# Rank-160 gate products with the activations stationary, split gate weights, and a re-drawn instruction order in a four-layer hybrid trunk

## The chip, the cores and the metric

The kernel runs on one core of one Trainium2 chip. The metric is the device time of one execution in microseconds (us); the time of a kernel is the median of its runs. TensorE's granted clock is 1.00 of full speed (2.4 GHz) in every stretch of the profile.

## The reference

The input x is 256 tokens by 1024 features in float32. Four layers follow each other; each is a token mixer and a SwiGLU feed-forward block, both with RMSNorm ahead and a residual add behind. The mixers are, in order, RWKV-7 (layer 0), stick-breaking attention (layer 1), top-64 sparse attention (layer 2) and RWKV-7 again (layer 3). What matters here, cut from the reference:

```
g = sigmoid(xg @ g1) @ g2                       # g1: 1024 x 160, g2: 160 x 1024, both RWKV layers
v = v + (v_first - v) * sigmoid(v0 + (xv @ v1) @ v2)    # v1: 1024 x 32, v2: 32 x 1024, layer 3 only
y = (groupnorm(y) + bonus) * g ; out = y @ w_out

# stick breaking: z = q k^T; att = exp(log_sigmoid(z) + sum of log_sigmoid(-z) over the later keys)
```

`xg` and `xv` are mixes of each token with the one before it. The RWKV recurrence is computed in chunks of 64 tokens, with a triangular inverse of each chunk.

## The kernel before, in words

Features lie on the 128 partitions, tokens (256) along the free axis. A float32 product that must be exact is done in one of two ways. Either both operands stay float32, and TensorE spends two MATMUL records on each product. Or the weight piece (128x1024, 512 KB) is split into a rounded float32r part `wh` and a rest `wl` (`piece`, line 825: one DMA into `raw`, one cast, one VectorE subtraction), the activation likewise, and three float32r products are summed (`mm3`). `raw`, `wh` and `wl` have three buffers each.

**The order** of all instructions on all engines is worked out in Python before the program is built. Every instruction is recorded as an operation with a cost; `Plan.schedule` (line 685) places them by list scheduling on a cost model, with the longest remaining path as priority, in 16 rounds (`ROUNDS`, line 221), and keeps the best. One more round then adds random shifts to the priorities of ranges of operations (`_nudge`, line 673), from a table of seeds, ranges and widths (`NUDGES`, line 223, 84 entries). An operation marked "any" goes to ScalarE or VectorE as the planner finds room. Where TensorE would be idle, the planner puts in small dummy products (tile `warm_o`).

**The gate in `rwkv`.** Its first weights lie in the tile `lora` (line 1034), which shares its memory with the later key tile `QC` (line 1181): `QC` can be written only when the gate's first products have read `lora`. For each of the 8 feature chunks, `g1a` (128 columns of g1) and `g1b` (the other 32, doubled to fill 64) are stationary and `xg` moves, 256 columns, in float32 (line 1142 on); in layer 3 the 64 columns of v1 (doubled) are a third product, on the other half of the array. The results are copied out to `sg` and go through a sigmoid. The second half (tile `pg`, line 1331 on) multiplies by g2: four DMAs of 128 KB and one of 256 KB fetch it (`lg`, `lg1`, lines 1259 and 1263), and for each of 4 pairs of chunks there are two full float32 products and two of 32 rows, four copies in all of 256 columns going to `gT`. `gT` is first used when the recurrence's output is scaled.

**What surrounds it.** In order of dependence: mixes; the products k (`kp`) and r (`rp`); the small products that make decay and rate; the keys `QC` (written twice by one VectorE instruction, line 1198: slots 0 and 2 hold the same values) and `PR`; scores `sc`, masked into `SB`; then a trip through DRAM (`scr`), 31 steps of a triangular inverse on VectorE (`inv`), back through DRAM (`scx`) into `XT`, whose two tiles take one `wh` and one `wl` buffer; `cmb` completes the inverse; then the chain of small products over the chunks (`xu`, `qu`, `Y`, `pS`), the norm, and the output product `po`. The value products `vp` and the gate's second half lie beside the inverse.

**In `stick`**, per head, two float32r products with the triangle `ntri` and one float32 product with `nones` (line 1543) make the sums over later keys.

Of the kernel before, what the change touches and what calls it, by code (L numbers as in the profile page):

```python
# [22 lines left out]
P = 128  # L23
# [4 lines left out]
C = 64  # L28
# [21 lines left out]
CONSTS = [("ident", 128), ("bones", 128), ("center", 128), ("mstrict", 64), ("mincl", 64),  # L50
# [138 lines left out]
class Queue:  # L189
# [33 lines left out]
NUDGES = [  # L223
# [21 lines left out]
]  # L245
# [64 lines left out]
class Plan:  # L310
# [362 lines left out]
    def _nudge(self):  # L673

        shift = collections.Counter()
        for seed, lo, hi, width in NUDGES:
            draw = random.Random(seed)
            for o in self.ops[max(lo, 0):hi]:
                d = draw.gauss(0.0, width)
                if draw.random() < 0.5:  # L680
                    shift[o] += d
        for o, d in shift.items():
            o.rank += d

    def schedule(self, counts):
# [6 lines left out]
        for k in range(ROUNDS + 1):  # L692
            if k == ROUNDS:
                order = [o for o, _, _ in basis]
                for o, start, end in basis:
                    o.start, o.end = start, end
            base = [(o, o.start, o.end) for o in order]
            self._place(counts, order)
            if k == ROUNDS:
                self._nudge()  # L700
# [4 lines left out]
            if r is None:  # L705
                break
# [46 lines left out]
def trunk(ctx: ExitStack, tc: tile.TileContext, xT_in, vecs_in, wts, lora_in, consts_in, id32_in, nqk_in, outT, order, layers=None):  # L753
# [96 lines left out]
    def split(h, l, src):  # L850
        anye.copy(h, src)
        dve.tensor_tensor(l, src, f(h), op=ALU.subtract)

# [179 lines left out]
    def rwkv(j, layer, after):  # L1033
        lw = T([4096], "QC", "lora")
        sp.dma_start(lw[:, :1024], lora_in[j][:, :1024])
        sp.dma_start(lw[:, 1024:], lora_in[j][:, 1024:4096])
        w1a1, l2 = v3(lw[:, :1024], 8), lw[:, 1024:2048]
        g1a, g1b = v3(lw[:, 2048:3072], 8), v3(lw[:, 3072:], 8)
# [103 lines left out]
        pga, pgb = bank("g1a"), bank("g1b")  # L1142
        for c in range(NC):
            xg = xm("mg", c)
            mixed = plan.ops[-1]
            if sv_:
                x = xm("mv", c)
                split(xv[0][:, c], xv[1][:, c], x)
            else:
                x = xv[:, c]  # L1150
                mix(x, "mv", c)
            with unit(1, 1010.0):
                pe.matmul(pga[:, :S], g1a[:, c, :], xg, start=(c == 0), stop=(c == NC - 1))
                pe.matmul(pgb[:64, :S], g1b[:, c, :64], xg, start=(c == 0), stop=(c == NC - 1))
                if j == 1:
                    pe.matmul(pgb[64:, :S], g1b[:, c, 64:], x, start=(c == 0), stop=(c == NC - 1))
        anye.copy(sga, pga[:, :S])
        anye.copy(sgb if j == 1 else sgb[:64], pgb[:, :S] if j == 1 else pgb[:64, :S])
# [25 lines left out]
        for p in range(0, NC, 2):  # L1184
# [13 lines left out]
            dve.tensor_tensor(pairs(QC, p)[:, :, ::2], c8(kk)[:, :, None].to_broadcast([P, 2 * NCH, 2, C]),  # L1198
                              c8(Ft[:, p:p + 2])[:, :, None].to_broadcast([P, 2 * NCH, 2, C]), op=ALU.mult)
# [58 lines left out]
        act.activation(sgb[:64], sgb[:64], AF.Sigmoid)  # L1258
        lg = [T([S], "xm", "lg") for i in range(4)]
        for i in range(4):  # L1260
            sp.dma_start(lg[i], lora_in[j][:, 4096 + i * S:4096 + (i + 1) * S])
            plan.after(plan.ops[-1], [mixed])
        lg1 = T([2 * S], "sqa", "lg1")
        sp.dma_start(lg1, lora_in[j][:, 5120:5120 + 2 * S])

        def second(out, p, r0, stop):

            r = slice(r0 + (p % 2) * 32, r0 + (p % 2) * 32 + 32)
            pe.matmul(out, lg1[r, (p // 2) * P:(p // 2 + 1) * P], sgb[r], start=(r0 > 0), stop=stop)

        for n in range(4):
# [7 lines left out]
            with unit(2):  # L1279
                for i in range(2):  # L1280
                    second(pv_[i][:, :S], 2 * n + i, 64, True)
# [49 lines left out]
        gT = T([NC, S], "s7", "gT")  # L1331
        for p in range(0, NC, 2):
            pg = bank("pg"), bank("pg")
            with unit():
                for i in range(2):
                    pe.matmul(pg[i][:, :S], lg[p // 2][:, i * P:(i + 1) * P], sga, start=True, stop=False)
                for i in range(2):
# [159 lines left out]
    def stick(layer, after):  # L1497
# [3 lines left out]
        msb, ntri = T([P], "kc0", "msb", BF16), T([P], "kc1", "ntri", F32R)  # L1501
        pool.tensor_copy(msb, cst("msb"))
        anye.copy(ntri, cst("ntri"))
        ohl = [T([2, 4, S], f"s{h}", "ohl", F32R) for h in range(2)]
# [5 lines left out]
        for p in range(8):  # L1510
# [22 lines left out]
            for hh in range(2):  # L1533
# [6 lines left out]
                with unit():  # L1540
                    pe.matmul(z[:, :W3], ntri, eh, start=False, stop=False, skip_group_check=True)
                    pe.matmul(z[:, :W3], ntri, el, start=False, stop=False, skip_group_check=True)
                    pe.matmul(z[:, P:S], cst("nones"), e[:, S:], start=False, stop=True, skip_group_check=True)
# [241 lines left out]
def _piece(d, key):  # L1785

    k = key[0]
    if k in "gu":
# [34 lines left out]
def _npieces(layers=None):  # L1823
    return sum({"rwkv": 32, "stick": 32, "dsa": 37, "ffn": 66}[k] for k, _ in _subs(layers))


def _lora(d, j):
# [4 lines left out]
    last = np.zeros((4, 32, PIECE), np.float32)  # L1832
    for k, w in enumerate((g2[128:], v2)):
        for i in range(2):
            last[2 * k + i, :, :D // 2] = w.reshape(32, NC, P)[:, i::2].reshape(32, D // 2)
    return np.concatenate([_rows(np.concatenate([w1, a1], 1), 0, 8, 0, 128), np.concatenate([w2, a2], 0),
                           _rows(g1, 0, 8, 0, 128), _rows(np.concatenate([g1[:, 128:], g1[:, 128:], v1, v1], 1), 0, 8, 0, 128),
                           g2[:128], last.reshape(P, PIECE)], 1)


NLORA = 1024 * 6
# [19 lines left out]
def _constants():  # L1861
# [25 lines left out]
    c["mincl"] = (i[:, None] % 64 <= t[None, :])  # L1887
    c["msb"] = np.where(i[:, None] >= i[None, :], NEG, 0.0)
# [43 lines left out]
```

## Time and profile before

| | us |
|---|---|
| median of 3 runs | 1411.22 |
| lowest and highest | 1411.19, 1411.52 |
| the profiled execution | 1412.52 |
| its span in the profile | 1410.7 |
| TensorE busy | 1393.9 (99%) |
| VectorE busy | 1113.3 (79%) |
| ScalarE busy | 740.6 (52%) |

Busy time of TensorE includes the dummy products, and the end of a pipelined matmul is modelled. Because the records of neighbouring matmuls overlap, the pace of a series is read from start to start, not from the duration of one. "PE" is TensorE's matmul, "PEld" its weight load, DVE is VectorE, ACT ScalarE, POOL GpSimd, SP the engine that issues the DMAs.

### The profile page before, as it was taken

The numbers are of one execution on the slowest core, as the hardware profiler recorded it, in microseconds if no ns is written. First come the engines' busy times: TensorE is split into PE (matmuls) and PEld (weight loads), VectorE is DVE, ScalarE is ACT, GpSimd is POOL, SyncE is SP. The second block draws the span as 40 slices with busy tenths as digits, with TensorE's granted clock in tenths as the row PEclk, the third lists the DMA queues.
The fourth block names the chain that finished last, engine by engine and source line by source line (L and its number), as shares of the span: only waits on it lengthen the run. The fifth ranks groups of instructions, "written<-read, shape, count | busy, mean of one in ns | idle before, by whom it ended". The sixth has DMA issues, their size and how long they took to land.

```text
span 1410.7 us, 25585 instructions
## 1 busy us (share of the span) xinstructions
PE 1393.9 (99%) x10196; PEld 1186.8 (84%) x10196; DVE 1113.3 (79%) x1954; ACT 740.6 (52%) x1258; POOL 8.6 (1%) x17
## 2 busy tenths in 40 slices
PE   9999999999999999999999999999999999999998
PEld 7787798888888898888887898888887877988887
DVE  7987588987677779886689888986599875888874
ACT  4734665444466755554466875443358156554432
POOL 0000000000000000000000000000001000000000
PEclk9999999999999999999999999999999999999999
DMA  6344046556565355565654455665444330555564
GB/s 237 124 125 141 10 135 192 181 181 200 171 185 164 105 154 191 194 192 187 204 168 148 165 164 171 195 193 187 137 138 124 120 106 17 165 182 179 190 190 140
DMA packets 78935, 224.10 MB, mean 159 GB/s; under 512 B 23776, under 2 KB 25184, under 8 KB 78560
## 3 DMA queue, kind: packets, MB, share of 16 engines
q1 hardware_dynamic: 78816, 222.47, 49.5%
q8 instruction: 80, 1.31, 0.4%
q14 instruction: 39, 0.32, 0.1%
HBM read 219.30 MB, written 3.15 MB: 158 GB/s over the span
## 4 chain that ended last, share of the span: by engine, by line
PE 92%; DVE 3%; DMA 3%; ACT 1%; SPq 1%; issue 0%; DVEq 0%; ACTq 0%
PE gate L749 18%; PE up L749 17%; PE dn L749 16%; PE po L749 6%; PE kp L749 4%; PE rp L749 3%; PE qk L749 3%; PE vps L749 3%; PE z L749 2%; PE vp L749 2%; PE q L749 2%; PE k L749 2%; DMA raw<-in_wts_dram 1%; PE sc L749 1%; PE Y L749 1%; PE attn_o L749 1%
## 5 line engine op out<-in xcount | busy, mean ns | idle before, releaser
L749 ACT CAST wh<-raw 128x1024 fp32r<-128x1024 f32 x336 | 350.6, 1050 | 390.0 <-PE dn L749 125.6
L749 DVE TENSOR_TENSOR wl<-raw,wh 128x1024 fp32r<-128x1024 f32 x373 | 449.9, 1220 | 73.3 <-ACT wh L749 65.6
L749 PE MATMUL gate<-xg,wh 128*128 128x512 f32 x704 | 255.5, 397 | 0.8 <-DVE gus L749 0.8
L749 PE MATMUL up<-xg,wh 128*128 128x512 f32 x704 | 255.8, 396 | 0.0
L749 PE MATMUL dn<-h,wh 128*128 128x512 f32 x704 | 247.2, 395 | 0.0
L749 PE MATMUL dn<-h,wl 128*128 128x256 f32 x704 | 197.3, 280 | 1.3 <-DVE wl L749 1.3
L749 PE MATMUL gate<-xg,wl 128*128 128x256 f32 x704 | 197.0, 280 | 0.0
L749 PE MATMUL up<-xg,wl 128*128 128x256 f32 x704 | 197.0, 280 | 0.0
L749 PEld LDWEIGHTS gate<-xg,wh 128*128 128x128 f32 x704 | 132.1, 188 | 32.6 <-PE up L749 1.3
L749 PEld LDWEIGHTS up<-xg,wh 128*128 128x128 f32 x704 | 132.1, 188 | 31.2
L749 PEld LDWEIGHTS dn<-h,wh 128*128 128x128 f32 x704 | 132.0, 188 | 30.9
L749 PEld LDWEIGHTS dn<-h,wl 128*128 128x128 f32 x704 | 132.9, 189 | 2.0 <-DVE wl L749 1.9
L749 PEld LDWEIGHTS gate<-xg,wl 128*128 128x128 f32 x704 | 132.8, 189 | 0.1
L749 PEld LDWEIGHTS up<-xg,wl 128*128 128x128 f32 x704 | 132.8, 189 | 0.1
L749 PE MATMUL vp<-xv,raw 128*128 128x256 f32 x256 | 59.6, 385 | 1.8 <-DMA raw<-in_wts_dram 1.5
L749 DVE TENSOR_TENSOR gus<-gus,rstd 128x512 f32<-128x512 f32 x88 | 59.8, 686 | 1.2
L749 DVE TENSOR_TENSOR xt<-xt,dn 128x256 f32<-128x256 f32 x64 | 26.6, 419 | 41.0 <-PE dn L749 40.3
L749 PEld LDWEIGHTS vp<-xv,raw 128*128 128x128 f32 x256 | 47.3, 190 | 10.1 <-DMA raw<-in_wts_dram 2.3
L749 PE MATMUL rp<-prx,wh 128*128 128x256 f32 x256 | 51.2, 299 | 0.0
L749 PE MATMUL po<-yhl,wh 128*128 128x256 f32 x256 | 49.4, 293 | 0.0
L749 PE MATMUL po<-ohl,wh 128*128 128x256 f32 x256 | 48.4, 289 | 0.0
L749 PE MATMUL qk<-xg,wh 128*128 128x512 f32 x128 | 46.5, 405 | 0.0
(300 smaller groups left out, 2354.3 us busy)
## 6 DMA issues: line engine op xcount, KB each, us to landing
raw<-in_wts_dram SPq DMA_DIRECT2D x397, 512.0 KB, 3.6
lora<-in_lora_dram SPq DMA_DIRECT2D x2, 1536.0 KB, 7.5
xt<-in_xT_dram SPq DMA_DIRECT2D x4, 256.0 KB, 3.9
lora<-in_lora_dram SPq DMA_DIRECT2D x2, 512.0 KB, 6.0
lg<-in_lora_dram SPq DMA_DIRECT2D x8, 128.0 KB, 2.4
inv<-in_id_dram SPq DMA_DIRECT2D x2, 512.0 KB, 3.6
scr<-SB SPq DMA_DIRECT2D x16, 64.0 KB, 1.9
inv<-scr SPq DMA_DIRECT2D x2, 512.0 KB, 3.2
```

What stands on the lines that cost most here:

```text
L749: getattr(getattr(nc, o.eng), method)(*map(real, args), **{k: real(a) for k, a in kw.items()})
```

## The change

Five edits, cut to their core:

1. **First gate products.** `xg` becomes the stationary operand (two blocks of 128 tokens), and all 160 columns of g1 move. The result has tokens on partitions; it is copied out in four pieces (the 32 last columns three times), transposed back by four TensorE transposes, and copied to `sg`. v1 (layer 3) becomes a product of its own: four chunks at once on four 32-column strips of the array, then summed by a product with a constant `sum4`.
2. **Second gate products.** g2 comes as two ordinary weight pieces, `lg` (split) and `lh` (its rows 128 to 159 three times over, made into rounded parts and rest); `sg` is split too. Per chunk there are three float32r products over 128 rows and one over 96 rows, and one 512-column copy per pair of chunks. The DMAs of `lg` and `lg1` go; layer 3 gets two small ones (`lv`) for v2. `lora` shrinks from 4096 to 3584 columns.
3. **Keys.** `QC` slot 0 is written by VectorE, and slot 2 copied from it by either engine.
4. **Stick sums.** `nones` and the moving operand are float32r: two products of 128 columns in place of one in float32.
5. **Planner.** The table `NUDGES` is new and longer (168 entries in place of 84, down to ranges of 3 operations), its shifts are uniform instead of Gaussian, and before that round each operation is put back to its base engine and cost.

```
-        pga, pgb = bank("g1a"), bank("g1b")
+        pgt = bank("g1")
+        pvl = bank("v1") if j else None
-            with unit(1, 1010.0):
-                pe.matmul(pga[:, :S], g1a[:, c, :], xg, start=(c == 0), stop=(c == NC - 1))
-                pe.matmul(pgb[:64, :S], g1b[:, c, :64], xg, start=(c == 0), stop=(c == NC - 1))
-                if j == 1:
-                    pe.matmul(pgb[64:, :S], g1b[:, c, 64:], x, ...)
+            with unit():
+                for b in range(2):
+                    pe.matmul(pgt[:, b * 160:b * 160 + 160], xg[:, b * P:(b + 1) * P], g1[:, c, :], ...)
+            if j == 1 and c % 4 == 3:
+                with unit(4):
+                    for i in range(4):
+                        pe.matmul(pvl[32 * i:32 * i + 32, :S], v1[:, c - 3 + i, :], xv[:, c - 3 + i], ...)
+        anye.copy(gt[:, :, :P], gp[:, :, :P])
+        for i in range(3):
+            anye.copy(gt[:, :, P + 32 * i:P + 32 * i + 32], gp[:, :, P:])
+            for b in range(2):
+                pe.transpose(gp[:, b * P:(b + 1) * P], gt[:, b, :P], cst("ident"))
+                pe.transpose(gp[:96, S + b * P:S + (b + 1) * P], gt[:, b, P:], cst("ident"))
...
+            anye.copy(part, pvl[:, :S])
+            pe.matmul(o[64:, :S], cst("sum4"), part, start=True, stop=True)
+            anye.copy(vl[64:], o[64:, :S])
...
-            dve.tensor_tensor(pairs(QC, p)[:, :, ::2], <kk, doubled>, <Ft, doubled>, op=ALU.mult)
+            dve.tensor_tensor(pairs(QC, p)[:, :, 0], c8(kk), c8(Ft[:, p:p + 2]), op=ALU.mult)
+            anye.copy(pairs(QC, p)[:, :, 2], pairs(QC, p)[:, :, 0])
...
+        split(gx[:, 0], gx[:, 1], sga)
+        plan.after(split3(gy, sgb, 64), [mixed])
...
+        wg = piece(("lg", j))
+        wraw, wy = raw_piece(("lh", j)), T([PIECE], "wh", "wy", F32R)
+        split3(wy, wraw, 32)
-                    pe.matmul(pg[i][:, :S], lg[p // 2][:, i * P:(i + 1) * P], sga, start=True, stop=False)
-                    second(pg[i][:, :S], p + i, 0, True)
-                anye.copy(gT[:, p + i, :], pg[i][:, :S])
+                    mm3(o[:, i * S:(i + 1) * S], [w[:, sl] for w in wg], (gx[:, 0], gx[:, 1]), i == 0, False)
+                    pe.matmul(o[:, i * S:(i + 1) * S], wy[:96, sl], gy[:96], start=False, stop=(i == 1))
+            anye.copy(gT[:, p:p + 2], ab(o))
...
-                    pe.matmul(z[:, P:S], cst("nones"), e[:, S:], ...)
+                    pe.matmul(z[:, P:S], nones, eh[:, S:], ...)
+                    pe.matmul(z[:, P:S], nones, el[:, S:], ...)
...
+    def split3(h, src, at):
+        anye.copy(h[:96], src[:96])
+        done = plan.ops[-1]
+        dve.tensor_tensor(h[at:at + 32], src[at:at + 32], f(h[at:at + 32]), op=ALU.subtract)
+        return done
```

## Rows read from the trace of the kernel before

**Rows 1.** The page's chain of work that ended last, by engine (share of the span).

```profile
PE 92%; DVE 3%; DMA 3%; ACT 1%; SPq 1%; issue 0%; DVEq 0%; ACTq 0%
```

**Rows 2.** Busy time by sublayer (a row's columns: stretch, its length, then busy us and instructions of PE, PEld, DVE, ACT, POOL, the granted clock, DMA share, GB/s). Shown are RWKV layer 0, its feed-forward block, the stick layer and RWKV layer 3.

```profile
0.00:203.50 203.50, 198.33 (x2163) 163.29 (x2164) 158.68 (x332) 114.17 (x234) 4.33 (x10) 1.00 0.41 128
203.50:390.90 187.40, 186.84 (x1062) 162.47 (x1061) 150.15 (x223) 87.03 (x117) 0.00 (x0) 1.00 0.58 184
390.90:508.40 117.50, 117.50 (x782) 102.14 (x781) 83.26 (x136) 78.32 (x148) 0.29 (x1) 1.00 0.47 147
1017.00:1219.20 202.20, 197.71 (x2179) 161.22 (x2180) 160.12 (x326) 113.82 (x238) 3.56 (x3) 1.00 0.35 104
```

**Rows 3.** The dummy products `warm_o` alone, by stretch (length, busy us of PE and instructions, clock, DMA share, GB/s).

```profile
0.00:20.00 20.00, 9.92 (x62) 1.00 0.84 299
...
1017.00:1060.00 43.00, 3.66 (x32) 1.00 0.39 123
...
sum 1411.00, PE 21.99; mean PE 1.47
```

**Rows 4.** TensorE's timeline in layer 0 (start, length of the merged records, tile, shapes, number of records): the last four chunks of the first gate products and the product `rp` behind them.

```profile
65.45 0.60 PE L749 MATMUL g1a<-xm,lora 128*128 128x256 f32 x2
...
70.17 0.51 PE L749 MATMUL rp<-prx,wh 128*128 128x256 f32 x2
```

**Rows 5.** TensorE's timeline in layer 3: five chunks of the first gate products, later three more, each group from its first record to the `rp` behind it.

```profile
1061.61 0.60 PE L749 MATMUL g1a<-xm,lora 128*128 128x256 f32 x2
...
1067.56 0.50 PE L749 MATMUL rp<-prx,wh 128*128 128x256 f32 x2
...
1077.27 0.60 PE L749 MATMUL g1a<-xm,lora 128*128 128x256 f32 x2
...
1080.80 0.51 PE L749 MATMUL rp<-prx,wh 128*128 128x256 f32 x2
```

**Rows 6.** TensorE's timeline in layer 3: sixteen full float32 products of 256 columns (two records each), then four records of 32-row products side by side, then the next tile.

```profile
1118.20 7.14 PE L749 MATMUL vp<-xv,raw 128*128 128x256 f32 x32 [0.33 <-DVE inv L749]
...
1125.28 0.70 PE L749 MATMUL pv<-sg,lg 32*128 32x256 f32 x4
...
1125.91 1.15 PE L749 MATMUL vtok<-consts,vf 64*64 64x64 f32 x32
```

**Rows 7.** Weight loads of the second gate products in layer 3, three pairs of chunks, to the tile behind them (merged records; the number in brackets is idle time ahead).

```profile
1149.07 0.73 PEld L749 LDWEIGHTS pg<-sg,lg 128*128 128x128 f32 x4
...
1150.76 0.73 PEld L749 LDWEIGHTS pg<-sg,lg 128*128 128x128 f32 x4 [0.33 <-ACT gT L749]
...
1154.14 0.30 PEld L749 LDWEIGHTS bn<-prhl,bonesr 128*128 128x128 f32 x2 [0.33 <-issue]
```

**Rows 8.** TensorE's timeline: four transposes of 128x128 in the sparse-attention layer, and what follows; and two heads' sums in the stick layer.

```profile
719.67 0.60 PE L749 MATMUL turned<-consts,turn 128*128 128x128 f32 x4
720.03 0.48 PE L749 MATMUL q<-wh,xg 128*128 128x512 f32 x1
...
462.50 0.60 PE L749 MATMUL z<-ehl,ntri 128*128 128x384 f32 x2
...
463.08 0.60 PE L749 MATMUL z<-ehl,ntri 128*128 128x384 f32 x2
```

**Rows 9.** A piece of the chain that ended last (start, length, work): 24 float32r products of 256 columns.

```profile
74.29 2.87 PE rp L749 x24
```

**Rows 10.** Groups of instructions over the whole span (engine, operation, tiles, shapes, count, busy us, mean ns of one, idle time before and its releaser).

```profile
L749 DVE TENSOR_TENSOR QC<-kk,EF 128x1024 f32<-128x1024 f32 x8 | 9.7, 1218 | 0.5 <-PE g1b L749 0.5
L749 DVE TENSOR_TENSOR QC<-k,EF 128x512 f32<-128x512 f32 x8 | 5.1, 684 | 0.0
L749 ACT COPY QC<-qct 128x512 f32<-128x512 f32 x15 | 8.0, 593 | 1.9 <-PE qct L749 1.8
L749 DVE TENSOR_TENSOR wl<-raw,wh 128x1024 fp32r<-128x1024 f32 x373 | 449.9, 1220 | 73.3 <-ACT wh L749 65.6 <-PE po L749 2.8
L749 ACT CAST wh<-raw 128x1024 fp32r<-128x1024 f32 x336 | 350.6, 1050 | 390.0 <-PE dn L749 125.6 <-PE up L749 85.3 <-PE gate L749 77.4
L749 ACT COPY gT<-pg 128x256 f32<-128x256 f32 x15 | 4.9, 374 | 5.5 <-PE pg L749 3.4 <-DMA scx<-inv 2.1
```

**Rows 11.** Busy time in stretches of 8 us (columns as in Rows 2): two of layer 0 ahead of the inverse, one in the recurrence.

```profile
56.00:64.00 8.00, 8.00 (x51) 6.09 (x51) 7.98 (x14) 6.93 (x14) 0.23 (x1) 1.00 0.30 104
...
88.00:96.00 8.00, 8.00 (x85) 7.01 (x85) 7.81 (x14) 1.52 (x3) 0.00 (x0) 1.00 0.12 20
...
152.00:160.00 8.00, 7.74 (x191) 6.26 (x187) 3.96 (x16) 3.00 (x10) 0.00 (x0) 1.00 0.01 2
```

**Rows 12.** Pieces of the chain that ended last in layer 0 (start, length, work).

```profile
97.63 1.92 DMA scr<-SB
...
126.96 4.62 DMA scx<-inv
...
138.33 0.62 PE cmb L749 x32
138.96 1.69 PE pg L749 x8
...
146.52 0.38 PE xu L749 x8
```

**Rows 13.** DMA issues (tile, engine, count, KB each, median us to landing).

```profile
raw<-in_wts_dram SPq DMA_DIRECT2D x397, 512.0 KB, 3.6
```

More of the change, by code (lines that the diff above doesn't have):

```diff
@@ L48 @@
 VIDX = {n: i for i, n in enumerate(VECS)}
-CONSTS = [("ident", 128), ("bones", 128), ("center", 128), ("mstrict", 64), ("mincl", 64),
+CONSTS = [("ident", 128), ("bones", 128), ("center", 128), ("mstrict", 64), ("mincl", 64), ("sum4", 64),
           ("ntri", 128), ("nones", 128), ("msb", 128),
@@ L221 @@
 ROUNDS = 16
-NUDGES = [
[21 rows of a table removed]
-]
+NUDGES = [[
[42 rows of a table added]
+]]
 WAIT = {"tensor": 85.0, "vector": 55.0, "scalar": 40.0, "gpsimd": 40.0, "sync": 0.0}
@@ L671, in _schedule, with _nudge @@
         return max(free.values()), sorted(out, key=lambda o: o.start)
-    def _nudge(self):
-        shift = collections.Counter()
-        for seed, lo, hi, width in NUDGES:
+    def _nudge(self, table):
+        for seed, lo, hi, width in table:
             draw = random.Random(seed)
             for o in self.ops[max(lo, 0):hi]:
-                d = draw.gauss(0.0, width)
+                d = width * (2.0 * draw.random() - 1.0)
                 if draw.random() < 0.5:
-                    shift[o] += d
-        for o, d in shift.items():
-            o.rank += d
+                    o.rank += d
     def schedule(self, counts):
@@ L691, in schedule @@
         order, best, basis = list(self.ops), None, None
-        for k in range(ROUNDS + 1):
+        for k in range(ROUNDS + len(NUDGES)):
             if k == ROUNDS:
@@ L696, in schedule @@
                     o.start, o.end = start, end
+            if k >= ROUNDS:
+                for o in self.ops:
+                    o.eng, o.cost = o.base
             base = [(o, o.start, o.end) for o in order]
             self._place(counts, order)
-            if k == ROUNDS:
-                self._nudge()
+            if k >= ROUNDS:
+                self._nudge(NUDGES[k - ROUNDS])
             for reserve in RESERVES:
@@ L1033, in rwkv @@
     def rwkv(j, layer, after):
-        lw = T([4096], "QC", "lora")
+        lw = T([3584], "QC", "lora")
         sp.dma_start(lw[:, :1024], lora_in[j][:, :1024])
-        sp.dma_start(lw[:, 1024:], lora_in[j][:, 1024:4096])
+        sp.dma_start(lw[:, 1024:], lora_in[j][:, 1024:3584])
         w1a1, l2 = v3(lw[:, :1024], 8), lw[:, 1024:2048]
-        g1a, g1b = v3(lw[:, 2048:3072], 8), v3(lw[:, 3072:], 8)
+        g1, v1 = v3(lw[:, 2048:3328], 8), v3(lw[:, 3328:], 8)
         rs = rstd_bcast(True)
@@ L1151, in rwkv @@
                 mix(x, "mv", c)
-            with unit(1, 1010.0):
-                pe.matmul(pga[:, :S], g1a[:, c, :], xg, start=(c == 0), stop=(c == NC - 1))
-                pe.matmul(pgb[:64, :S], g1b[:, c, :64], xg, start=(c == 0), stop=(c == NC - 1))
-                if j == 1:
-                    pe.matmul(pgb[64:, :S], g1b[:, c, 64:], x, start=(c == 0), stop=(c == NC - 1))
-        anye.copy(sga, pga[:, :S])
-        anye.copy(sgb if j == 1 else sgb[:64], pgb[:, :S] if j == 1 else pgb[:64, :S])
+            with unit():
+                for b in range(2):
+                    pe.matmul(pgt[:, b * 160:b * 160 + 160], xg[:, b * P:(b + 1) * P], g1[:, c, :],
+                              start=(c == 0 and b == 0), stop=(c == NC - 1 and b == 1))
+            if j == 1 and c % 4 == 3:
+                with unit(4):
+                    for i in range(4):
+                        pe.matmul(pvl[32 * i:32 * i + 32, :S], v1[:, c - 3 + i, :], xv[:, c - 3 + i], start=(c == 3), stop=(c == NC - 1))
+        gt = flat(t2("gt"))[:, :448].rearrange("p (b k) -> p b k", b=2)
+        gp = pgt[:, :320].rearrange("p (b k) -> p b k", b=2)
+        anye.copy(gt[:, :, :P], gp[:, :, :P])
+        for i in range(3):
+            anye.copy(gt[:, :, P + 32 * i:P + 32 * i + 32], gp[:, :, P:])
+        gp = bank("g1t")
+        with unit():
+            for b in range(2):
+                pe.transpose(gp[:, b * P:(b + 1) * P], gt[:, b, :P], cst("ident"))
+                pe.transpose(gp[:96, S + b * P:S + (b + 1) * P], gt[:, b, P:], cst("ident"))
+        anye.copy(sga, gp[:, :S])
+        anye.copy(sgb[:96], gp[:96, S:])
+        if j == 1:
+            part, vl, o = t1("vpart"), t1("vl"), bank("v1s")
+            anye.copy(part, pvl[:, :S])
+            pe.matmul(o[64:, :S], cst("sum4"), part, start=True, stop=True)
+            anye.copy(vl[64:], o[64:, :S])
         Dt, dc = T([NC, NCH, C + 1], "s6", "Dt"), T([NC, NCH], "dc", "dc")
@@ L1257, in rwkv @@
         act.activation(sga, sga, AF.Sigmoid)
[L1258 to L1269, printed above, removed]
+        act.activation(sgb[:96], sgb[:96], AF.Sigmoid)
+        gx = T([2, S], "sqa", "gx", F32R)
+        split(gx[:, 0], gx[:, 1], sga)
+        gy = T([S], "xm", "gy", F32R)
+        plan.after(split3(gy, sgb, 64), [mixed])
+        if j == 1:
+            lv = [T([S], "xm", "lv") for i in range(2)]
+            for i in range(2):
+                sp.dma_start(lv[i][64:], lora_in[j][64:, 3584 + i * S:3584 + (i + 1) * S])
+                plan.after(plan.ops[-1], [mixed])
         for n in range(4):
@@ L1280, in rwkv @@
                 for i in range(2):
-                    second(pv_[i][:, :S], 2 * n + i, 64, True)
+                    r = slice(64 + 32 * i, 96 + 32 * i)
+                    pe.matmul(pv_[i][:, :S], lv[n // 2][r, (n % 2) * P:(n % 2 + 1) * P], vl[r], start=True, stop=True)
             sv, d_ = t2("sv"), t2("vd")
@@ L1331, in rwkv @@
         gT = T([NC, S], "s7", "gT")
+        wg = piece(("lg", j))
+        wraw, wy = raw_piece(("lh", j)), T([PIECE], "wh", "wy", F32R)
+        split3(wy, wraw, 32)
         for p in range(0, NC, 2):
-            pg = bank("pg"), bank("pg")
-            with unit():
-                for i in range(2):
-                    pe.matmul(pg[i][:, :S], lg[p // 2][:, i * P:(i + 1) * P], sga, start=True, stop=False)
-                for i in range(2):
-                    second(pg[i][:, :S], p + i, 0, True)
-            for i in range(2):
-                anye.copy(gT[:, p + i, :], pg[i][:, :S])
+            o = bank("pg")
+            for i in range(2):
+                sl = slice((p + i) * P, (p + i + 1) * P)
+                with unit():
+                    mm3(o[:, i * S:(i + 1) * S], [w[:, sl] for w in wg], (gx[:, 0], gx[:, 1]), i == 0, False)
+                    pe.matmul(o[:, i * S:(i + 1) * S], wy[:96, sl], gy[:96], start=False, stop=(i == 1))
+            anye.copy(gT[:, p:p + 2], ab(o))
         def combine(p):
@@ L1500, in stick @@
         load_consts(1, sbu[:, 3072:3072 + CSPLIT[2] - CSPLIT[1]])
-        msb, ntri = T([P], "kc0", "msb", BF16), T([P], "kc1", "ntri", F32R)
+        msb, ntri, nones = T([P], "kc0", "msb", BF16), T([P], "kc1", "ntri", F32R), T([P], "kc2", "nones", F32R)
         pool.tensor_copy(msb, cst("msb"))
         anye.copy(ntri, cst("ntri"))
+        anye.copy(nones, cst("nones"))
         ohl = [T([2, 4, S], f"s{h}", "ohl", F32R) for h in range(2)]
@@ L1542, in stick @@
                     pe.matmul(z[:, :W3], ntri, el, start=False, stop=False, skip_group_check=True)
-                    pe.matmul(z[:, P:S], cst("nones"), e[:, S:], start=False, stop=True, skip_group_check=True)
+                    pe.matmul(z[:, P:S], nones, eh[:, S:], start=False, stop=False, skip_group_check=True)
+                    pe.matmul(z[:, P:S], nones, el[:, S:], start=False, stop=True, skip_group_check=True)
                 act.activation(at[:, hh], z[:, :W3], AF.Exp)
@@ L1787, in _piece @@
     k = key[0]
+    if k in ("lg", "lh"):
+        g2 = d["rw_g2"][key[1]]
+        return g2[:P] if k == "lg" else _pad(np.concatenate([g2[P:]] * 3), D)
     if k in "gu":
@@ L1823, in _npieces @@
 def _npieces(layers=None):
-    return sum({"rwkv": 32, "stick": 32, "dsa": 37, "ffn": 66}[k] for k, _ in _subs(layers))
+    return sum({"rwkv": 34, "stick": 32, "dsa": 37, "ffn": 66}[k] for k, _ in _subs(layers))
 def _lora(d, j):
@@ L1831, in _lora @@
     g1, g2, v1, v2 = d["rw_g1"][j], d["rw_g2"][j], d["rw_v1"][0], d["rw_v2"][0]
[L1832 to L1835, printed above, removed]
+    last = np.zeros((4, 32, 2 * S), np.float32)
+    for i in range(2):
+        last[2 + i] = v2.reshape(32, NC, P)[:, i::2].reshape(32, D // 2)
     return np.concatenate([_rows(np.concatenate([w1, a1], 1), 0, 8, 0, 128), np.concatenate([w2, a2], 0),
-                           _rows(g1, 0, 8, 0, 128), _rows(np.concatenate([g1[:, 128:], g1[:, 128:], v1, v1], 1), 0, 8, 0, 128),
-                           g2[:128], last.reshape(P, PIECE)], 1)
-NLORA = 1024 * 6
+                           _rows(g1, 0, 8, 0, 160), _rows(v1, 0, 8, 0, 32), last.reshape(P, 2 * S)], 1)
+NLORA = 4096
 def _vectors(d):
@@ L1887, in _constants @@
     c["mincl"] = (i[:, None] % 64 <= t[None, :])
+    c["sum4"] = (i[:, None] % 32 == i[None, :64] % 32)
     c["msb"] = np.where(i[:, None] >= i[None, :], NEG, 0.0)
```

4 lines of the change are left out of this document (removed), and 63 rows, old and new, of the table NUDGES.

## The prediction, on record before the result was known

> **What bounds the kernel now.** I read the chain of waits first, then busy time by sublayer, then the timeline of each tile that the change touches. The chain lies 92% on TensorE [rows 1]. By sublayer TensorE is busy without a gap in the stick layer and in the feed-forward blocks, and idle for 5.2 us of layer 0's mixer (203.50 less 198.33) and 4.5 us of layer 3's (202.20 less 197.71) [rows 2]. Some of the busy time is dummy products: 22.0 us in all, of which 9.9 fill the start and 3.7 the entry of layer 3 [rows 3]. So beside the two entries there are 5.2 + 4.5 + (22.0 - 9.9 - 3.7) = 18.1 us that a better order could still find; everything else is TensorE's own work, and a product made shorter should show in the end time, unless another resource is as full. In RWKV one is: ahead of the inverse VectorE is busy 7.98 and 7.81 of 8 us beside a full TensorE [rows 11]. Behind that lies a path that no product shortens: the scores go out to DRAM at 97.63, VectorE's 31 steps end at 126.96, the way back takes 4.62, and the first `cmb` stands at 138.33, some 41 us [rows 12].
>
> **First gate products.** Four chunks took 70.17 - 65.45 = 4.72 us, 1.18 a chunk, 9.4 for the eight of layer 0 [rows 4]. In layer 3 the eight took 5.95 + 3.53 = 9.5 us [rows 5]. That is much for two products: sixteen full float32 products of 256 columns in a row take 1125.28 - 1118.20 = 7.08 us, 0.44 each [rows 6]. The alternation of a full-width and a half-width product costs the rest. The change moves 160 columns past a full-width operand twice per chunk. No row has such a product; by columns it is 0.44 x 160/256 = 0.28, at worst the whole 0.44, below nothing not. I take 0.28, since the series of rows 6 runs at its columns' pace: 16 x 0.28 = 4.4. The four transposes take 0.36 together, as four did in 720.03 - 719.67 [rows 8]. New total 4.8; layer 0 saves 4.6 us. Layer 3 has v1 besides: two sets of four products on four strips, each taken as the side-by-side set of 32-row products, 1125.91 - 1125.28 = 0.63 [rows 6], and the `sum4` product at the same price: 1.9 us, so that it saves 9.5 - 6.7 = 2.8. If the strips did not run side by side, eight products at 0.44 would cost 3.5 and 2.3 us of that would go.
>
> **Second gate products.** Three pairs of chunks took 1154.14 - 1149.07 = 5.07 us, 1.69 each [rows 7]. A pair becomes eight float32r products of 256 columns; 24 of them took 2.87 us, 0.12 each [rows 9], so 0.96. Saved: 0.73 x 4 = 2.9 a layer, 5.8 in both. That one in four of them has 96 rows I cost at nothing: the row for a smaller product (32 rows, 0.63 for two) is float32.
>
> **Stick sums.** A head takes 463.08 - 462.50 = 0.58 us [rows 8]; two float32r products of 384 columns are by columns 0.36 of it [rows 9], so the float32 one is 0.22. Its two float32r heirs of 128 columns cost between 0.06 (by columns) and 0.12 each (the pace of 256). I take the 0.09 of a transpose, the nearest row of 128 columns [rows 8]: 0.04 saved in each of 16 heads, 0.6 in all, with ends of +1.6 and -0.3.
>
> **TensorE in sum:** 4.6 + 2.8 + 5.8 + 0.6 = 13.8 us less work.
>
> **VectorE and ScalarE.** The doubled key write of 1.218 us becomes one of 0.684 [rows 10]: 8 x 0.53 = 4.3 us off VectorE, in the stretch in which it is full. The copy, 0.59 on ScalarE [rows 10], is hidden there (1.52 of 8 us busy [rows 11]). Added to each layer on VectorE: two subtractions for the weight pieces at 1.22, two for `sg` at no more than 0.68 each, 3.8 us; on ScalarE two casts of 1.05 and small copies, less four pairs of `gT` copies (eight of 0.374 become four of 0.59) [rows 10]. I cost these at nothing: `gT` is not due until the recurrence, where VectorE is busy 3.96 of 8 us [rows 11]. Without that cover 3.8 us per layer stand inside the inverse, on the path.
>
> **Queue and buffers.** SP issues two 512 KB pieces instead of five smaller transfers per layer, and `lora` shrinks by 256 KB: the same bytes. A piece lands in 3.6 us [rows 13]. The wait that the change adds is on weight buffers: `XT`, `lg` and `wy` hold the three `wh`, so the first output pieces can be loaded only after the last `pg`. That is nothing if the gate is finished before the recurrence starts, and 3.6 + 1.05 + 1.22 = 5.9 us per layer if it is finished just when `po` wants its weights. I take nothing, since the gate's inputs exist long before.
>
> **What of it arrives.** Ahead of the inverse, layer 0 frees 4.6 us on TensorE and 2.1 on VectorE, both full there; `QC` lies where `lora` lay, so the gate's products stay in this stretch. I take 3.0, between the two, because the planner may hand a few casts from VectorE to ScalarE. Layer 3 frees 2.8 and 2.1: 2.1. In the inverse, `pg` frees 2.9 a layer; TensorE still does `pg` after the first `cmb` (138.96), and the chain starts at 146.52 [rows 12], so that work can move ahead of it: 2.0 of the 2.9 each. Stick: 0.6. Together 3.0 + 2.1 + 4.0 + 0.6 = 9.7. The longer table works on the 18.1 us above; I take a sixth, 3.0, and as bounds half of it won or lost (9). Sum 12.7: the profiled execution's 1412.52 becomes 1399.8. It lies 1.3 above the median of the runs, so the forecast is **1398.5**.
>
> **Rivals.** (1) *The gain is hidden.* TensorE's freed time in RWKV turns into dummy products, because VectorE and the inverse end last. Then only VectorE's 4.3 and the stick's 0.6 arrive: 1411.2 - 4.9 = 1406.3. For it: rows 11 and 12. Against: TensorE is as full in the same stretch. (2) *Slower: VectorE's new work falls on the inverse.* An in-order VectorE that does the gate's subtractions between the 31 steps, and the key copies too, delays `scx` by 3.8 us per layer, with TensorE waiting at `cmb`: 1411.2 + 7.6 = 1418.8. It decides once the four subtractions stand ahead of the last step. For it: the planner works by modelled costs. Against: they are due 40 us later than the inverse. (3) *The weight loads show.* If the load of the stationary `xg` were not hidden behind 160 columns, each of 64 records would grow by its load, 0.15 (two in 0.30 [rows 7]): 9.6 us lost, 1408.1. Rows 6 speak against: sixteen products with their 32 loads run at 0.44 each. The Trainium skill, "TensorE: Matmul & The Clock Gate", Part 3, says that a weight load overlaps matmuls in flight only where the row groups differ, and here they are the same; by that the sum would lose these 9.6 us. The trace's full-row series contradicts it for 256 columns; for 160 no run here shows it yet.
>
> **How the numbers follow.** The forecast's case gets 0.67, with a range of its own of 1390 to 1404 (half of the table's 18.1 us won; the worse ends for the 160-column products and v1, some 5 us of TensorE). Rival 1 gets 0.17, rival 2 gets 0.10, rival 3 gets 0.06. The range of 1389 to 1409 holds the first, rival 1 and rival 3 with most of their spread, and leaves out rival 2. A difference of 0.2%, 2.8 us, is about what a measurement of this kernel can tell from no change. Faster by more: 0.67 and most of rival 1 and half of rival 3, 0.80. Within it: the rest of these and rival 2's mild end, 0.11. Slower: 0.09.
>
> **What would show it.** Right: a chunk of first gate products at some 0.56 us instead of 1.18; a pair of `pg` at some 0.96; the key write at 0.68; RWKV layers shorter by some 5 to 7 us (layer 0) and 4 to 6 (layer 3), the feed-forward blocks unchanged, and dummy products and idle time not larger than now. Wrong: the stages as long as before with more `warm_o` (rival 1); gate subtractions among the steps of `inv` and a `cmb` that waits for `XT` (rival 2); 160-column records 0.3 us apart (rival 3); or a loss in the stick layer or the feed-forward blocks, which the new order may bring and of which no row of before gives the size.

## The result, and the profile after

The median is **1398.79 us** (five executions, 1395.47 to 1402.63), against 1411.22 us for the kernel before beside it (1410.19 to 1414.53): a ratio of 0.991, with a 95% interval of 0.9886 to 0.9933. Measured again beside the experiments it gave 1396.58 us and 0.9886 (0.9868 to 0.9905). So the change saves 12 to 16 us, and the forecast of 1398.5 us holds. The profiled execution is the median one: 1398.79 us, with a span of 1397.0 us, 13.7 us shorter than before.

The chain still lies on TensorE, with a little more of it on VectorE than in [rows 1]. This is its row by engine on the page of after:

```profile
PE 91%; DVE 4%; DMA 3%; ACT 1%; SPq 1%; issue 0%; ACTq 0%; DVEq 0%
```

Busy time by sublayer, columns as in [rows 2], the stick layer counted from the last record of `dn`, the feed-forward block's last product, as there: RWKV layer 0, its feed-forward block, the stick layer, the second feed-forward block with sparse attention, the third feed-forward block, and RWKV layer 3.

```profile
0.00:194.80 194.80, 189.97 (x2166) 164.67 (x2167) 159.06 (x338) 117.72 (x239) 3.73 (x10) 1.00 0.41 132
194.80:382.40 187.60, 187.60 (x1067) 163.09 (x1066) 148.05 (x218) 93.35 (x122) 0.00 (x0) 1.00 0.59 189
382.40:499.30 116.90, 116.70 (x778) 101.42 (x778) 85.49 (x142) 75.95 (x144) 0.34 (x1) 1.00 0.44 145
499.30:822.90 323.60, 323.60 (x1898) 274.62 (x1897) 270.26 (x506) 180.84 (x317) 0.27 (x2) 1.00 0.54 175
822.90:1010.00 187.10, 187.10 (x1065) 162.88 (x1063) 147.97 (x224) 80.18 (x101) 0.12 (x1) 1.00 0.57 184
1010.00:1205.40 195.40, 189.61 (x2181) 161.61 (x2180) 164.29 (x340) 114.92 (x238) 2.74 (x3) 1.00 0.35 109
```

Layer 0 is 8.7 us shorter than in [rows 2] and layer 3 is 6.8 shorter. The first feed-forward block (187.6 against 187.4) and the stick layer (116.9 against 117.5) are as long as before. The stretch behind them, 321.2 us before, is 2.4 longer, though TensorE is busy without a gap in it both times. The dummy products, columns as in [rows 3], have not grown:

```profile
0.00:20.00 20.00, 9.98 (x62) 1.00 0.77 273
...
1010.00:1050.00 40.00, 3.66 (x32) 1.00 0.36 115
...
sum 215.00, PE 21.32; mean PE 4.26
```

They come to 21.3 us against 22.0. The idle time of layer 0 comes to 4.8 against 5.2, that of layer 3 to 5.8 against 4.5. TensorE's busy time over the span falls by 12.4 us, from 1393.9 to 1381.5, and the span by 13.7. So the time that TensorE no longer needs did leave the program.

**The edits one by one.** TensorE's timeline in layer 3 shows two chunks of the first gate products together and one alone, each followed by `rp`, which answers to [rows 5]:

```profile
1056.93 1.25 PE L768 MATMUL g<-lora,xm 128*128 128x160 f32 x8
1057.91 0.51 PE L768 MATMUL rp<-prx,wh 128*128 128x256 f32 x2
...
1059.45 0.71 PE L768 MATMUL g<-lora,xm 128*128 128x160 f32 x4
1059.89 0.51 PE L768 MATMUL rp<-prx,wh 128*128 128x256 f32 x2
```

From start to start a chunk takes 0.98/2 = 0.49 or 0.44 us, where it took 1.18; some 0.1 more stands at the first `rp` behind it, whose two records take 0.35 instead of 0.24. With it a chunk costs some 0.54, near the 0.56 of the prediction, though a product by itself is cheaper than its 0.28 (0.22 to 0.25) and the 0.1 was not in its sum. The chain of waits in layer 0 has 24 records, that is three pairs, of the second gate products, and the first `cmb`, for [rows 7, 12]:

```profile
130.09 3.07 PE pg L768 x24
133.17 0.62 PE cmb L768 x32
```

A pair takes 1.02 us instead of 1.69. Two heads of the stick layer, for [rows 8]:

```profile
453.78 0.51 PE L768 MATMUL z<-ehl,ntri 128*128 128x384 f32 x2
454.13 0.33 PE L768 MATMUL z<-ehl,nones 128*128 128x128 f32 x2
454.30 0.56 PE L768 MATMUL z<-ehl,ntri 128*128 128x384 f32 x2
454.70 0.33 PE L768 MATMUL z<-ehl,nones 128*128 128x128 f32 x2
454.87 0.45 PE L768 MATMUL qk<-xg,wh 128*128 128x512 f32 x1
```

They take 0.52 and 0.57 us against 0.58. The groups over the whole span, for [rows 10]: the key write, its copy, and the copies of `gT`.

```profile
L768 DVE TENSOR_TENSOR QC<-kk,EF 128x512 f32<-128x512 f32 x8 | 5.5, 684 | 0.0
L768 ACT COPY QC<-QC 128x512 f32<-128x512 f32 x7 | 4.3, 619 | 3.5 <-DVE QC L768 3.5
...
L768 ACT COPY gT<-pg 128x512 f32<-128x512 f32 x8 | 4.5, 586 | 2.4 <-PE pg L768 2.2
```

Each edit does what it says, at nearly the predicted price. Whether those prices explain the time is what the experiments ask.

### The profile page after: what moved, and what is told of

The parts are those of the page before. It is cut to its first block, busy times and chain, and to the rows that moved or that the text cites. A ratio compares the mean times of both kernels' runs of the same rounds, so it can differ in the third digit from the quotient of the medians.

```text
span 1397.0 us, 25605 instructions
## 1 busy us (share of the span) xinstructions
PE 1381.5 (99%) x10204; PEld 1190.5 (85%) x10204; DVE 1118.2 (80%) x1970; ACT 743.3 (53%) x1269; POOL 7.2 (1%) x17
## 4 chain that ended last, share of the span: by engine, by line
PE 91%; DVE 4%; DMA 3%; ACT 1%; SPq 1%; issue 0%; ACTq 0%; DVEq 0%
PE dn L768 17%; PE up L768 17%; PE gate L768 17%; PE po L768 7%; PE rp L768 3%; PE vps L768 3%; PE qk L768 3%; PE kp L768 3%; PE z L768 2%; DMA raw<-in_wts_dram 2%; PE vp L768 2%; PE q L768 2%; PE k L768 2%; PE sc L768 1%; PE Y L768 1%; PE attn_o L768 1%
## 5 line engine op out<-in xcount | busy, mean ns | idle before, releaser
L768 ACT CAST wh<-raw 128x1024 fp32r<-128x1024 f32 x329 | 344.2, 1051 | 366.7 <-PE dn L768 123.5
L768 DVE CAST wh<-raw 128x1024 fp32r<-128x1024 f32 x46 | 31.7, 690 | 19.7 <-PE dn L768 8.4
```

The source lines that it names most:

```text
L768: getattr(getattr(nc, o.eng), method)(*map(real, args), **{k: real(a) for k, a in kw.items()})
```

## The experiments

The theory (W below): TensorE and VectorE work that is removed arrives in the end time, and the table adds a little. Its rivals: the freed time is hidden by something else, or it is the table and the order (O) that bring the gain.

**The changed kernel again**, as an anchor for the runs measured beside it.

> The changed kernel once more, on the chip on which the kernels with extra work run, as their base: ratio to the kernel before 0.991, some 1398 to 1399.

1396.58 us, 0.9886 (0.9868 to 0.9905).

**The tables taken away.** Three runs: the changed kernel and the kernel before each without a table, and the changed kernel with every seed raised by one, which leaves the planner with the best order of its sixteen plain rounds: TensorE's records are those of the first run, in the same order, up to the 9198th of 10230. So the third run is nearly the first once more, and shows nothing of how good an order by other shifts is.

```
-NUDGES = [[ (645776, 2423, 2431, 3000), ... ]]
+NUDGES = [[]]                                  # first run
+NUDGES = []                                    # second run, on the kernel before
+        draw = random.Random(seed + 1)         # third run
```

> The changed kernel with an empty table of shifts: the same products, the plain planner's order. Theory W (the time went because TensorE has 12.8 us less work; the order matters little): about 3 us above the changed kernel, some 1402, ratio to the kernel before 0.993. Rival O (the time went because the longer table found a better order): 1408 to 1412, ratio 0.998 to 1.000.

> The kernel before with an empty table. Against e1 it gives the worth of the other four edits under the plain planner, and against the kernel before the worth of the old table. Theory W: the old table is worth about as much as the new one, 2 to 4 us, so 1413 to 1415, and 11 to 14 us above e1. Rival O: the old table is worth nothing to 1 us (1411 to 1412), and the distance to e1 is under 4 us.

> The changed kernel with each seed of its table raised by one: the same ranges and widths, other shifts, none of them chosen. It shows how far an order by chance lies from the chosen one. Theory W: the planner keeps the best of its rounds by its own cost, so at worst as e1, some 1402 (1399 to 1405). Rival O: as e1 would be under O, 1408 or more.

The changed kernel without a table: 1411.96 us, 0.9989 (0.9973 to 1.0006). The kernel before without one: 1418.52 us, 1.0035 (1.0022 to 1.0048). Other seeds: 1410.28 us, 0.9985 (0.997 to 1.0). So W was wrong here: without its table the changed kernel is no faster than the kernel before, as rival O had it. The second run fits neither: O had the old table worth at most 1 us and the two kernels within 4, W had them 11 to 14 apart. Like against like, the four other edits bring 1.0035 - 0.9989 = 0.46%, some 6.5 us, in one order of each kernel; by the intervals this is known to about 3 us. The old table was worth 4.9 us, and the new one is worth 11 (0.9989 to 0.991) to 15 (to 0.9886).

The profiles say where the 6.5 stop and what the table does with them. These are starts read from the timelines, layer 0 from the start of the span, layer 3 from the last `dn` record ahead of it:

| us | first inverse step | first `cmb` | end of layer |
|---|---|---|---|
| layer 0: before, no table | 105.9 | 140.4 | 206.2 |
| before | 102.9 | 138.3 | 203.4 |
| changed, no table | 100.7 | 138.1 | 204.1 |
| changed, half the table | 99.9 | 134.0 | 200.3 |
| changed | 99.7 | 133.1 | 194.8 |
| layer 3: before, no table | 99.5 | 140.1 | 203.6 |
| before | 99.7 | 140.9 | 202.6 |
| changed, no table | 95.4 | 134.3 | 200.8 |
| changed, half the table | 94.7 | 135.1 | 196.4 |
| changed | 96.0 | 135.6 | 196.0 |

Without tables, the edits bring the inverse of layer 0 forward by 5.2 us, and 2.3 of that are left at the first `cmb`. The chain of waits of the changed kernel without a table shows what takes them:

```profile
125.81 5.58 DMA scx<-inv
...
132.90 4.12 DMA XT<-scx
...
137.31 0.72 DVE xd L725
```

In the kernel before without a table, the same place of the chain is TensorE's own work, though there the way from the issue of the inverse's write to the first read back takes as long (134.56 - 129.26 = 5.3 us):

```profile
137.64 1.69 PE pg L727 x8
139.33 1.09 PE bv L727 x32
140.42 0.62 PE cmb L727 x32
```

```profile
129.26 0.33 SPq L727 DMA_DIRECT2D scx<-inv  x1
134.56 4.04 SPq L727 DMA_DIRECT2D XT<-scx  x8
```

The shorter `pg` no longer covers the way back through DRAM, and that way is long. SP's queue of the changed kernel without a table shows a likely reason: a 512 KB weight piece goes out half a microsecond ahead of the inverse.

```profile
125.30 0.33 SPq L725 DMA_DIRECT2D raw<-in_wts_dram  x1
125.81 0.33 SPq L725 DMA_DIRECT2D scx<-inv  x1
131.47 5.43 SPq L725 DMA_DIRECT2D XT<-scx  x8
```

From the issue of the inverse's write to the first read back are 131.47 - 125.81 = 5.7 us. SP's queue of the changed kernel with its table:

```profile
124.04 0.33 SPq L768 DMA_DIRECT2D scx<-inv  x1
126.80 4.42 SPq L768 DMA_DIRECT2D XT<-scx  x8
131.33 10.35 SPq L768 DMA_DIRECT2D raw<-in_wts_dram  x5
```

Here no weight piece goes ahead, the same way takes 2.8 us, and the pieces follow when the last read of `XT` is issued. Its VectorE shows the end of the inverse and the first transpose of `XT`:

```profile
123.80 0.22 DVE L768 TENSOR_TENSOR inv<-inv,xtmp 128x31 f32<-128x31 f32 x1
124.05 1.21 DVE L768 TENSOR_TENSOR wy<-raw,wy 32x1024 fp32r<-32x1024 f32 x1
...
130.92 1.30 DVE L768 STREAM_TRANSPOSE xd<-XT 128x512 f32<-128x512 f32 x2 [1.18 <-DMA XT<-scx]
```

From the last step to the transpose are 6.9 us; without a table it is 137.31 - 125.79 = 11.5, with VectorE idle for 6.03 of it. The other orders fit: with half the table no piece goes ahead and the write takes 2.65 us, with other seeds one goes 0.4 us ahead and it takes 5.7; in the kernel before, a piece went out some 2 us ahead, and it took 4.7 (1.6 us ahead and 5.3 without its table). The Trainium skill, "DMA: Bandwidth & Descriptors", Queues, rings and completion order, says that all transfers that SP issues go through one row of rings, one per DMA engine, each consumed in order; by that a piece issued just ahead is taken up first, and these profiles agree. Whether the piece holds the write up in the queue or only shares the DMA engines with it, no run tells. None moved this one piece alone, so its share of the table's worth is read from profiles, not isolated: of the 5.0 us that the table brings to the first `cmb` of layer 0, 1.0 stands ahead of the inverse, 0.8 in its steps (25.1 us against 24.3), and the rest here. In layer 3 the table's gain lies behind the first `cmb` (66.5 us to the end without a table, 60.4 with it), 4.3 of it in idle time and dummies (8.7 us against 4.3), and 3.4 us without a table run at half clock; no single wait there stands for it.

**The first gate products made longer.** To each unit of the first gate products come dummy products, 10.3 us in all, the order kept.

```
+            plan.ops[-1].fill = 3          # three pairs of dummy products behind each unit
```

> The changed kernel in its own order, with six dummy products of 256 columns behind each of the 16 chunks of the first gate products: 96 x 0.107 = 10.3 us of TensorE work put back where the change took some out (7.2 us). Theory W: the time grows by 8 to 10.5 us. Rival H (ahead of the inverse VectorE ends last and TensorE's time is hidden): by 0 to 3 us.

1408.06 us, 0.9964 (0.9951 to 0.9977): 11 us over the changed kernel beside it, a little more than expected. W holds: TensorE has no slack in this stretch. The inverse of layer 0 starts at 105.1, 5.4 later.

**The second gate products made longer**, by the same line behind each chunk of `pg`, 10.3 us (some 9.5 by its trace).

> The changed kernel in its own order, with twelve dummy products of 256 columns behind each of the 8 pairs of the second gate products: 96 x 0.107 = 10.3 us. Theory W: the time grows by 7 to 10.5 us. Rival H (the way of the inverse through VectorE and DRAM ends last): by 0 to 3 us.

1404.59 us, 0.9937 (0.9922 to 0.9951): 7 us more. About three quarters of what is put beside the inverse arrives.

**The key write done three times**, the order kept. The expectation put this at 9.6 us more for VectorE ahead of the inverse; by the traces the writes grow from 5.5 to 16.5 us, 11.1 more.

```
+            plan.ops[-1].again = 2
```

> The changed kernel in its own order, with the key write of 0.68 us done three times in place of once: 8 x 2 x 0.6 = 9.6 us more on VectorE ahead of the inverse. If VectorE has no room there (as its 7.8 to 8.0 of 8 us say), the time grows by 6 to 10 us, and the halved key write was worth some 4 us of the gain by itself; under theory W alone (TensorE ends last) it grows by 0 to 3 us.

1408.49 us, 0.997 (0.9957 to 0.9983): 12 us more, over the 6 to 10 expected, and the inverse of layer 0 starts at 104.5, 4.7 later. VectorE binds there as hard as TensorE does [rows 11].

**The kernel before with less work, its order kept.** First, `g1b` (and v1) are left out in chunks 1 to 6; then the 32-row second gate products are left out. The expectations put this at 8.8 and 6.3 us of TensorE; followed end to end, the records of these products fall by 8.2 (18.4 to 10.2) and 5.0 (13.3 to 8.3).

```
+            if 0 < c < NC - 1:
+                plan.ops[-1].cut = (1, 2)  # first run
+            plan.ops[-1].cut = (2, 3)      # second run
```

> The kernel before in its own order, its half-width first gate products (g1b, in layer 3 also v1) left out in chunks 1 to 6 of 8, so that those columns of the gate are sums over two chunks alone. A chunk should fall from 1.18 to some 0.45 us: 12 x 0.73 = 8.8 us less on TensorE, nothing re-planned. Theory W: faster by 5 to 9 us. Rival H: by 0 to 3 us, with more idle time on TensorE before the inverse.

> The kernel before in its own order, with the 32-row products of the second gate products left out (the last 32 of its 160 columns do not count): a pair falls from 1.69 to some 0.9 us, 8 x 0.79 = 6.3 us less on TensorE, nothing re-planned. Theory W: faster by 3 to 6 us. Rival H: by 0 to 2 us.

1406.04 us, 0.9947 (0.993 to 0.9964), and 1409.37 us, 0.9971 (0.9961 to 0.9981): 7.5 and 4 us saved of the 8.2 and 5.0 that the traces show. Removed TensorE work arrives by some 0.9 ahead of the inverse and by some 0.8 beside it, in the order of the old table and with nothing re-ordered.

**Is it the clock?** The granted clock of the changed kernel without its table is lower (0.992 to 1.000 over its executions; the kernel before without one has 0.999 to 1.000), and it was not expected. Busy time (columns as in [rows 2]) of the changed kernel without a table:

```profile
136.00:140.00 4.00, 2.42 (x84) 2.04 (x79) 1.30 (x2) 2.21 (x5) 0.00 (x0) 0.92 0.61 157
140.00:150.00 10.00, 10.00 (x152) 6.82 (x152) 5.82 (x9) 3.52 (x12) 0.00 (x0) 0.52 0.48 161
```

TensorE waits for the transposes of `XT` for 1.6 of 4 us, and then 10.2 us run at 1.2 GHz instead of 2.4. Of its twelve executions, the six with a mean clock of 0.998 or more have a mean of 1408.8 us, the six below 1413.8. So three more runs: dummy products put just ahead of those waits, in the order without a table; half the table; and the changed kernel with no dummy products after the first 20 us.

```
+FILL = {634: 8, 5397: 6, 5595: 4}          # first run: pairs of dummies behind these operations
+            for _ in range(FILL.get(n, 0)):
+                warmer()
-NUDGES = [[ <168 entries> ]]
+NUDGES = [[ <the first 84> ]]              # second run
+                if o.start < 30000.0:      # third run
+                    warmer()
```

> The changed kernel without a table, its order and its own dummy products kept, with 36 dummy products more (some 3.9 us of TensorE at full clock) at three places just ahead of the idle times that its profile shows in front of the two half-clock stretches (a 1.58 us wait of cmb for xd near 138 us, a 1.36 us wait of vp for raw near 1115 us, a 1.47 us hole in cmb near 1158 us). Theory C, the fallen clock is part of what the missing table costs: the granted clock comes back to 0.998 or more and the time falls from 1412 to 1406 to 1409.5 us. Theory O, the order alone costs it and the half-clock stretches lie where TensorE has slack: 1411 to 1416 us, whatever the clock does.

> The changed kernel with the first 84 of its 168 entries of shifted priorities, as many as the kernel before had. Theory L, the table's worth grows with its length: 1403 to 1407 us, between the 1412 without a table and the 1398.8 with the whole of it. Rival H, the first half already gives what the chip can use: 1397 to 1401 us. Rival N, only the whole list fits this kernel: 1409 to 1413 us.

> The changed kernel with its whole table and its order kept, all dummy products after the first 20 us left out (some 11 us of TensorE time by the profile). Theory C, the dummies hold the clock in the two RWKV stretches and lie in time that nothing else could use: the granted clock falls under 0.995 and the time rises by 3 to 8 us, to 1401 to 1407 us. Rival, this order needs them no more: the clock stays at 0.998 or more and the time stays at 1396 to 1399 us, or falls by up to 3 us.

*More dummies, no table:* 1411.12 us, 0.9982 (0.9972 to 0.9992); mean clock of the twelve executions 0.9993, where it was 0.9967. The profiled execution is the slowest of them (1415.34 us, clock 0.996); the same stretches in it:

```profile
136.00:140.00 4.00, 4.00 (x94) 3.22 (x90) 1.17 (x2) 1.96 (x4) 0.00 (x0) 1.00 0.75 190
140.00:150.00 10.00, 9.01 (x190) 6.75 (x189) 6.37 (x11) 5.22 (x18) 0.00 (x0) 0.83 0.44 150
```

Even here TensorE no longer idles in the first stretch, and 3.4 us run at half clock behind it instead of 10.2. The clock came back in most executions, the time did not: 0.8 us less, inside the intervals. So theory C falls as it was put. The 36 dummies (3.9 us as expected) may themselves have cost part of what the clock gave. The executions at a clock of 1.0 give an idea of the size: 1405.5 us without them (one execution), a mean of 1409.1 with them (six), still 7 and 10 us over the changed kernel. That speaks for the order as the larger part of what the missing table costs: here too the first `cmb` stands at 138.0, and the weight piece goes out 0.4 us ahead of the inverse.

*Half the table:* 1403.37 us, 0.9936 (0.9923 to 0.995). L holds: some 7.5 us from the first 84 entries (0.9989 to 0.9936), and 4 to 7 from the rest. The first half already takes the weight piece away from the inverse, and the first `cmb` comes to 134.0.

*No late dummies:* 1406.0 us, 0.9948 (0.993 to 0.9966), with granted clocks from 0.985 (1409.84 us) to 0.993 (1401.44 us). Its busy time in two stretches of layer 0:

```profile
136.00:140.00 4.00, 2.25 (x66) 1.75 (x64) 2.16 (x3) 3.10 (x6) 0.00 (x0) 0.83 0.40 162
140.00:160.00 20.00, 20.00 (x336) 17.04 (x331) 7.14 (x24) 7.42 (x25) 0.00 (x0) 0.50 0.18 54
```

and the same two of the changed kernel:

```profile
136.00:140.00 4.00, 4.00 (x95) 3.02 (x96) 2.33 (x3) 3.49 (x9) 0.00 (x0) 1.00 0.31 125
140.00:160.00 20.00, 19.37 (x462) 15.10 (x462) 10.19 (x33) 11.77 (x37) 0.00 (x0) 1.00 0.19 57
```

Here C holds. In the first, TensorE is idle for 1.75 of 4 us, the next 20 us run at half clock and get through 336 records in place of 462; layer 0 ends at 204.2 instead of 194.8. The dummy products are not waste in this order: of the 18.1 us that the prediction gave a better order to find, 8.4 are dummies, and leaving out all dummies after the first 20 us loses time.

## Why the prediction was right, and where it was not

**TensorE's work, 13.8 us: right.** The records of the first gate products, followed end to end over the whole span, fall from 18.4 to 11.2 us, 7.2 against a predicted 7.4. The second fall from 13.3 to 8.5, 4.8 against 5.8: a pair costs 1.02 to 1.07 with its entry, not 0.96. The sums of all 16 heads in the stick layer fall from 9.3 to 9.0, 0.3 against 0.6. Together 12.3, as much as TensorE's busy time fell.

**VectorE's cost ahead of the inverse: right.** The inverse of layer 0 starts 3.2 us earlier, against 3.0; that of layer 3 starts 3.7 earlier, where 2.1 were taken (5.2 and 4.1 when neither kernel has a table). The run with the key written three times shows why neither engine alone sets this: each has no room.

**What costs nothing: nearly right for VectorE, wrong for SP's queue.** The subtraction into `wy` stands at 124.05, right behind the last inverse step, and VectorE afterwards still waits 1.18 us for `XT`: it is covered. One of the small subtractions for `sg` is not: in layer 0 it stands at 88.99, among the masks of the scores, where VectorE is busy 7.58 of 8 us, and takes 0.42. The way back was read too short: the 4.62 us of [rows 12] are the inverse's write alone, and from the last step to the first `cmb` stand 138.33 - 126.96 = 11.4. And the new weight pieces were costed only at the same bytes and at the wait for their buffers. Their *place* in SP's queue was not looked at, and the inverse takes 2.8 us to DRAM where none goes just ahead of it, and 5.7 where one does.

**What of it arrives, 9.7, and the table, 3.0: both mis-sized, in opposite directions.** These are the terms of the sum that failed. Without tables 6.5 us arrive by the medians, not 9.7: layer 0 is 2.1 us shorter (206.2 to 204.1) where the sum had 5.0, layer 3 is 2.8 shorter where it had 4.1. In layer 0 the way back through DRAM ends last once `pg` is short; TensorE waits 1.6 us for it, and 10.2 us at half clock follow. No run separates the two: the six executions with a clock of 0.998 or more stand 9.7 us below the kernel before without a table, so the fallen clock may hold much of what is missing. The tables bring a net 6 to 10 us, not 3.0: 11 to 15 for the new one, less 4.9 for the old. The bound of 9 for the table lies inside that. The forecast of 12.7 in all was met by luck, because the two errors cancel; the mechanism of each edit was right, the split was not.

**The rivals.** Rival 1, the gain hidden behind VectorE and the inverse, is not what the changed kernel does, but without its table about half of the freed time does not arrive: the path that the prediction described in [rows 12] takes over at the first `cmb`. Its form there was the DMA on the way back, not VectorE's steps. Rival 2 did not occur: the 31 steps take 24.3 us from 99.73, and the `wy` subtraction follows them. Rival 3 did not occur. The weight loads of the first gate products (shortest, median and longest in ns, then the first and last start):

```profile
L768 PEld LDWEIGHTS g<-lora,xm x64: 187/190/192, 53.7 to 1066.9; 128*128 128x128 f32 x64
```

A load lasts 0.19 us, the records follow each other at 0.98/8 = 0.12 us, and TensorE waited for none of them. The rule of the Trainium skill, "TensorE: Matmul & The Clock Gate", Part 3, that loads overlap only where the row groups differ, is contradicted, read by itself, at 160 columns as it was at 256.

**Gain and loss by layer.** The RWKV layers are shorter by more than the 5 to 7 and 4 to 6 us that were named, by 8.7 and 6.8. A loss elsewhere was named as possible: the stick layer has none (from the last `dn` it takes 117.0 us against 117.5, and 118.8 to 118.9 in both kernels without a table), the stretch behind it has 2.4. That stretch varies from 321 to 326 us among all these orders, with TensorE idle for at most 1.2 us of it. What paces it was not found.

## What to carry to other kernels

Price a removed instruction at the engine that is full where it stands: here 0.8 to 1.1 of the time of added or removed work arrived, with the order kept. Then ask which path ends last once it is gone, and look at what its DMAs queue behind: where a bulk weight load went out half a microsecond ahead of the transfer on the critical path, the way back was 3 us longer (read from profiles, not isolated). And where an order is tuned to a program by search, the search is a term of its own: compare both programs without their tables, since the old one's table was lost with the change and the new one's bought more than all the other edits.

## What was not expected of the hardware

TensorE's granted clock fell from 2.4 to 1.2 GHz inside the RWKV layers, for 10.2 us in the order without a table and for 27.3 us without the late dummy products, the longest falls of the two profiles, each right behind a stretch of small products in which TensorE had been idle for 1.6 and 1.75 of 4 us. In the changed kernel's profiled execution it stays at 1.00, though its own executions vary with it: 1402.63 us at 0.995 against 1395.47 at 0.998.

The price of a fall depends on what ends last behind it: 27 us at half clock, with two more stretches of 6.8, go with 5 to 9 us of time (0.9948 against 0.991 and 0.9886); taking 0.003 of the mean clock back in the order without a table moved the median by 0.8.
